# A hybrid attention and RWKV-7 block on one core: the same traced instructions, put in order by the scheduler's timeline simulation

## The chip, the cores and the metric

The kernel runs on one core of a Trainium2 chip. The metric is the device time of one execution in microseconds (us). Five engines work beside each other, each through its own instructions in a fixed order: TensorE (PE; its weight loads are shown apart as PEld), VectorE (DVE), ScalarE (ACT), GpSimd (POOL) and SyncE (SP), which here only issues DMAs. An instruction that waits holds back all that stand behind it on its engine. What order they stand in is decided when the program is built.

## The reference

One layer over x of shape (1, 2048, 1024), all in float32, cut to what is computed:

```python
h    = rms_norm(x, pre_mix_g)
proj = h @ w_in                     # 1024 -> 1536 (q,k,v) + 1792 (rwkv) + 2048 (gates)
y_a  = chunk_band_attention(q, k, v, rel_bias)      # 8 heads of 64; own chunk of 64 + 8 before
y_b  = rwkv7_time_mix(p_rwkv, ...)                  # 8 heads of 64; token shift, decay, and a scan:
#   state = state * w_t + (state @ a_t) b_t^T + v_t k_t^T ;  y_t = state @ r_t
merged = sigmoid(g_a) * (y_a @ proj_a) + sigmoid(g_b) * (y_b @ proj_b)
x = x + rms_norm(merged @ w_out, post_mix_g)
u = square(relu(rms_norm(x, pre_ffn_g) @ w_up)) @ w_down
x = x + rms_norm(u, post_ffn_g)
```

## The kernel before

**Groups.** The 2048 tokens are worked on in four groups of 512 (`G`). `run` does for each group: `phase_rwkv`, `phase_attention`, `phase_merge`, with the norm of the next group (`phase_norm`, through `after`) beside the merge. Then come the feed-forward stages, `phase_up` and `phase_down`, each twice for half of the tokens.

**Fillers.** Products are made in three passes of split operands (`mm3`, L75): each operand is the sum of a high and a low part, made by `split` (L66 on ACT, the low part L67 on DVE). `dense` makes 128 columns of the combined projection: it loads a block of weights (`wsplit`, L60 on SP), splits it (tiles `whi`, `wlo`, two buffers each), and runs 24 matmuls of 512 columns into a PSUM tile `psd` (two buffers). `gate` is such a block with a tanh behind it, `branches` multiplies by `proj_a` or `proj_b` (tile `ps_p`). Apart from their weights and buffers these matmuls depend on nothing that is under way beside them.

**RWKV, per group.** The eight heads are worked on in four pairs, two pairs at a time, as two batches.
- `rwkv_pre` makes r, k, v, the decay and the scaled operands of a pair. At its end stand the steps L411 to L424 on DVE and the matmuls `ps_A` (L470), whose evictions L479 fill the tile NA.
- `rwkv_inverse` inverts 32x32 triangular blocks by 31 pairs of small DVE steps (L503, L509) and ends in two transposes on DVE (L512, L514).
- `rwkv_blocks` needs them: `ps_t1` (L533, shown as `ps_t`), a copy on ACT (L535), `ps_t2` (L540, also shown as `ps_t`), copies on ACT (L519, L521, L542).
- `rwkv_trans` goes on for each pair in steps that each need the one before: `ps_at` (L557), `ps_w` (L564), `ps_ug` (L574), `ps_tq` (L585), `ps_s0` (L598), `ps_y` (L602), with copies on ACT and DVE between them.
- `rwkv_chunk` carries the state through eight chunks: `ps_st` (L613), then L616 on DVE, then the next `ps_st`. `rwkv_post` norms the result: L627 on ACT, L629 on DVE, L630 and L632 on POOL, L634 on DVE, then the transposes `ps_yt` (L641).

**Attention, per group.** Four pairs of heads; `att_pair` makes q, k and v by three `dense` calls, evicted by L772 to L792, and then eight blocks of 128 queries. A block is `ps_s` (scores, L817, four matmuls of 320 columns from group 1 on), `sc` on DVE (bias and minimum, L823), exp on ACT (L828), reciprocal and scaling on DVE (L830, L831), `ps_pt` (five transposes, L835), the split of those into `PTh` on ACT (L839) and `PTl` on DVE (L840). For two blocks together come twelve matmuls `ps_pv` (L847) and the sum `ya` (L850). `ps_s` and `ps_pt` have one buffer each.

**What sets the order.** The source calls the pieces in an order laid out by hand: `GATES` and `STEPS` (L33, L34) say how many gates, or how many steps of a recurrence, are called at each `between()` inside `rwkv_pre`, and `phase_rwkv` and `phase_merge` place further pieces. All calls are recorded under a `TileContext`. When it closes, a scheduler puts the recorded instructions of each engine in order: it goes through the program on a simulated machine, gives each engine, when that engine is free, the earliest recorded instruction that is ready and has its buffers, and adds the semaphores. So the simulated machine's durations decide which of two ready pieces of work goes first. In the kernel before, that machine is the default one.

## Time and profile before

| | us |
|---|---|
| median of 3 runs | 3445.39 |
| lowest and highest | 3442.23, 3445.48 |
| the profiled execution | 3440.76 |
| its span | 3439.0 |
| busy: PE / DVE / ACT / POOL | 3298.4 / 2412.6 / 1414.1 / 420.2 |
| mean granted clock of TensorE | 0.987 |

How its rows are read. Busy time is the union of an engine's instructions; a matmul's duration contains its way through the array, so the distance between the starts of two neighbours tells the rate. A row of a list of groups has line, engine, operation, tiles, sizes and count, then busy time and the mean of one in ns, then idle time ahead and what ended it. A row of the stretches has the stretch and its length, then for PE, PEld, DVE, ACT and POOL busy time and count, then the granted clock (1.00 is full), the share of the DMA engines and GB/s. A row of the timeline has start, duration, engine, line, operation and tiles, how many are merged, and in brackets the idle time ahead and what ended it. A row of the waits has the waiting engine and line, what it waited for, and the sum, the count and the longest wait.

The stretches of the span are these: the first norm and the setup to about 30 us; then four groups of some 510 us, of which RWKV takes about the first 270, attention the next 150, and the merge with the next norm the rest; the feed-forward part from about 2080 us to the end.

### The profile page before, as it was taken

What the parts mean: (1) busy time and instruction counts of PE and PEld (TensorE: products, weight loads), DVE (VectorE), ACT (ScalarE), POOL (GpSimd) and SP (SyncE); (2) the same over time, 40 slices, a digit from 0 to 9 for tenths busy, and PEclk for the clock granted to TensorE, in tenths of its full rate; (3) what the DMA queues carried; (4) which work ended last, traced back from release to release, by engine and by line L of the source; (5) the groups of instructions that cost most, each with busy time, mean ns of one, the idle gap of its engine ahead of it and who ended that gap; (6) DMA issues with size and microseconds to landing.
All of it is one profiled execution on the core that took longest, in us unless ns stands there. A gap on an engine that the chain in (4) does not pass through costs nothing. (4 is left out here: it accounts for less than half of the span.)

```text
span 3439.0 us, 50370 instructions
## 1 busy us (share of the span) xinstructions
PE 3298.4 (96%) x19233; PEld 2674.2 (78%) x19233; DVE 2412.6 (70%) x4110; ACT 1414.1 (41%) x2319; POOL 420.2 (12%) x796
## 2 busy tenths in 40 slices
PE   7999999999989999999999989999999999999998
PEld 5777777777867777877777877888788878888886
DVE  5774856766865775865775875877877788776667
ACT  4434634436644445644435634333331243331112
POOL 2210002111022110012210000111200021100001
PEclk9999999999999999999999999999999999999999
DMA  5223353225373225373224376434845374343333
GB/s 146 84 87 126 133 204 97 60 86 190 120 267 113 65 93 168 124 263 123 80 84 141 96 254 229 129 120 141 293 157 185 98 242 133 118 144 98 98 98 110
DMA packets 397864, 481.10 MB, mean 140 GB/s; under 512 B 17516, under 2 KB 304432, under 8 KB 397624
## 3 DMA queue, kind: packets, MB, share of 16 engines
q1 hardware_dynamic: 346168, 364.63, 33.4%
q0 software_dynamic: 23040, 79.71, 6.1%
q10 hardware_dynamic: 28416, 33.56, 2.8%
q8 instruction: 151, 2.47, 0.3%
q14 instruction: 89, 0.73, 0.1%
HBM read 356.16 MB, written 124.81 MB: 140 GB/s over the span
## 5 line engine op out<-in xcount | busy, mean ns | idle before, releaser
L75 PE MATMUL ps_dn<-fop 128*128 128x512 f32 x3072 | 702.6, 390 | 3.6 <-DVE u L1170 3.5
L75 PEld LDWEIGHTS ps_dn<-fop 128*128 128x128 f32 x3072 | 576.7, 188 | 125.9 <-DVE u L1170 5.8
L75 PE MATMUL psd<-hh,whi 128*128 128x512 f32 x1344 | 545.6, 406 | 14.5 <-ACT whi L66 13.6
L75 PE MATMUL psd<-hl,whi 128*128 128x512 f32 x1344 | 544.0, 405 | 0.0
L75 PE MATMUL psd<-hh,wlo 128*128 128x512 f32 x1344 | 540.9, 402 | 1.9 <-DVE wlo L67 1.8
L66 ACT CAST whi<-wraw 128x1024 fp32r<-128x1024 f32 x232 | 243.3, 1049 | 522.8 <-PE psd L75 416.7
L1170 DVE TENSOR_TENSOR u<-u,ps_dn 128x512 f32<-128x512 f32 x480 | 323.2, 685 | 148.6 <-PE ps_dn L75 147.9
L67 DVE TENSOR_TENSOR wlo<-wraw,whi 128x1024 fp32r<-128x1024 f32 x232 | 282.9, 1220 | 189.6 <-ACT whi L66 171.1
L75 PEld LDWEIGHTS psd<-hh,whi 128*128 128x128 f32 x1344 | 258.4, 192 | 68.7 <-ACT whi L66 15.5
L75 PEld LDWEIGHTS psd<-hh,wlo 128*128 128x128 f32 x1344 | 258.1, 192 | 54.0 <-DVE wlo L67 5.0
L75 PEld LDWEIGHTS psd<-hl,whi 128*128 128x128 f32 x1344 | 258.2, 192 | 50.5
L66 ACT CAST fop<-wdraw 128x1024 fp32r<-128x1024 f32 x64 | 67.0, 1047 | 425.7 <-DVE u L1170 303.3
L1091 POOL DMA_DIRECT2D ad<-r x128 | 69.2, 541 | 588.5 <-DVE r L1090 572.4
L960 PE MATMUL ps_o<-whi,mh 128*128 128x512 f32 x256 | 103.1, 410 | 15.4 <-ACT whi L66 10.0
L75 PE MATMUL ps_p<-yh,whi 128*128 128x512 f32 x256 | 103.0, 402 | 12.0 <-DVE th L931 6.7
L66 ACT CAST s12h<-s 128x1024 fp32r<-128x1024 f32 x32 | 33.7, 1055 | 184.5 <-PE ps_u L75 184.5
L823 DVE CUSTOM_DVE_ANT_0 sc<-bias,ps_s 128x640 f32<-128x640 f32 (+4 forms) x128 | 93.4, 730 | 22.6 <-PE ps_pt L835 18.4
L828 ACT ACTIVATE sc<-sc,mn 128x640 f32<-128x640 f32 (+4 forms) x128 | 97.7, 764 | 19.3 <-DVE mn L823 18.7
L839 ACT CAST PTh<-ps_pt 128x640 fp32r<-128x640 f32 (+4 forms) x128 | 79.9, 624 | 59.3 <-PE ps_pt L835 55.0
L75 PE MATMUL ps_p<-yl,whi 128*128 128x512 f32 x256 | 102.9, 402 | 0.0
L75 PE MATMUL ps_p<-yh,wlo 128*128 128x512 f32 x256 | 102.8, 402 | 0.0
L1089 ACT ACTIVATE r<-r 128x512 f32<-128x512 f32 x128 | 80.7, 630 | 53.3 <-DVE r L1088 53.1
(352 smaller groups left out, 6659.6 us busy)
## 6 DMA issues: line engine op xcount, KB each, us to landing
wraw<-in_w_in_dram SPq DMA_DIRECT2D x168, 512.0 KB
wraw<-in_w_up_dram SPq DMA_DIRECT2D x80, 512.0 KB
ad<-r POOLq DMA_DIRECT2D x128, 256.0 KB, 2.4
wdraw<-in_w_down_dram SPq DMA_DIRECT2D x64, 512.0 KB
araw<-ad SPq DMA_DIRECT2D x64, 512.0 KB
gd<-gate ACTq DMA_DIRECT2D x64, 256.0 KB
th<-gd SPq DMA_DIRECT2D x32, 512.0 KB
wraw<-in_w_out_dram SPq DMA_DIRECT2D x32, 512.0 KB
```

What stands on the lines that cost most here:

```text
L66: self.nc.scalar.copy(hi, src)
L67: self.nc.vector.tensor_tensor(lo, src, hi.bitcast(F32), ALU.subtract)
L75: mm = nc.tensor.matmul(ps, l, r, start=n == 0, stop=n == last).ins
L823: nc.vector.tensor_tensor_reduce(sc[:, 0:n], bias[:, s0:640], pss[:, c0 : c0 + n], 1.0, 3.0e38, ALU.add, ALU.min, mn,)
L828: nc.scalar.activation(sc[:, 0:n], sc[:, 0:n], AF.Exp, scale=-1.0, bias=mn, accum_out=sm)
L839: nc.scalar.copy(hv, pst[:, 0:nk])
L960: nc.tensor.matmul(ps[t], l[:, k, ts], r[:, k % 2], start=k == 0 and j == 0, stop=k == KB - 1 and j == 2)
L1089: nc.scalar.activation(r, r, AF.Relu)
L1091: nc.gpsimd.dma_start(self.ad[fb][:, th], r)
L1170: nc.vector.tensor_tensor(u[t][:, ns], u[t][:, ns], ps, ALU.add)
```

## The change

```diff
-    with tile.TileContext(nc) as tc:
+    with tile.TileContext(nc, schedule_with_timeline_sim=True) as tc:
```

One argument is added. The recorded instructions, their operands, tiles and buffers are the same. The scheduler goes through them on another simulated machine, one with a timeline of each engine and its own durations, so it meets other instructions ready at other times, and each engine's order comes out differently. The program's semaphores follow the new order. Three places show how.

**PE in an attention stage.** The first piece is from the attention of group 1 before, between two sets of transposes `ps_pt` and beyond; `psd` rows are dense matmuls for later pairs.

```order
L835 MATMUL ps_pt<-ident,sc 128x128 x5
L75 MATMUL psd<-hl,whi 128x512
L817 MATMUL ps_s<-KK,QA 128x320
L817 MATMUL ps_s<-KK,QB 128x320
L817 MATMUL ps_s<-KK,QA 128x320
L817 MATMUL ps_s<-KK,QB 128x320
L847 MATMUL ps_pv<-PTh_7790,VV 128x256 x5
L847 MATMUL ps_pv<-PTl_7791,VV 128x256
L75 MATMUL psd<-hh,wlo 128x512
L75 MATMUL psd<-hh,whi 128x512
L75 MATMUL psd<-hl,whi 128x512
L847 MATMUL ps_pv<-PTl_7791,VV 128x256 x5
```

The same kind of place in the same stage now, four blocks into a pair:

```order
L835 MATMUL ps_pt<-ident,sc 128x128 x5
L847 MATMUL ps_pv<-PTh_7790,VV 128x256 x5
L847 MATMUL ps_pv<-PTl_7791,VV 128x256
L817 MATMUL ps_s<-KK,QA 128x320
L817 MATMUL ps_s<-KK,QB 128x320
L817 MATMUL ps_s<-KK,QA 128x320
L817 MATMUL ps_s<-KK,QB 128x320
L847 MATMUL ps_pv<-PTl_7791,VV 128x256 x5
L835 MATMUL ps_pt<-ident,sc 128x128 x5
```

Before, dense matmuls stand between the links of a block; now one set of transposes follows the other with the block's own matmuls alone, and the dense ones stand in long rows ahead of or behind such runs.

**PE behind the inverse.** The first inverse of group 0 before, from the end of `ps_t1`'s filler to `ps_at` (`ps_t_1387` is `ps_t2`):

```order
L75 MATMUL psd<-hh,wlo 128x512
L75 MATMUL psd<-hh,whi 128x512
L540 MATMUL ps_t_1387<-XT,Z 32x32
L75 MATMUL psd<-hl,whi 128x512
L75 MATMUL psd<-hh,wlo 128x512
L540 MATMUL ps_t_1387<-XT,Z 32x32 x31
L557 MATMUL ps_at<-ident,AR 128x128 x4
L75 MATMUL psd<-hh,whi 128x512
```

And now, from `ps_t1` (`ps_t_1352`) on:

```order
L533 MATMUL ps_t_1352<-X_1181,NA 32x32 x32
L540 MATMUL ps_t_1387<-XT,Z 32x32 x32
L557 MATMUL ps_at<-ident,AR 128x128 x8
L564 MATMUL ps_w<-SV,AR 64x64 x16
L574 MATMUL ps_ug<-WA,XT 64x128 x16
L602 MATMUL ps_y<-SV,BR 64x64
L585 MATMUL ps_tq<-BR,GT 64x128 x8
```

Twelve dense matmuls stood between `ps_t1` and the first `ps_t2` and more behind them; now none stands in this chain.

**DVE inside the first inverse.** A piece of the same inverse now, among the small steps L503 and L509:

```order
L509 TENSOR_TENSOR X<-X,T 128x24x4
L411 TENSOR_TENSOR tk<-tk,k 128x512
L412 SCALAR_TENSOR_TENSOR ta<-ta,k 128x512
L503 TENSOR_TENSOR T<-N,X 128x115
L421 TENSOR_TENSOR BK<-tk,Ei 64x8x64 x2
L424 SCALAR_TENSOR_TENSOR r<-r,cst,tk 128x512
L418 SCALAR_TENSOR_TENSOR BK<-ta,hkk,Ei 64x8x64 x2
L509 TENSOR_TENSOR X<-X,T 128x23x5
```

Before, the end of the same inverse read:

```order
L509 TENSOR_TENSOR X<-X,T 128x16
L293 SCALAR_TENSOR_TENSOR v<-pr,cst,v 128x512
L512 STREAM_TRANSPOSE X_1181<-X 128x32x16
L514 STREAM_TRANSPOSE XD<-X_1181 128x512
L411 TENSOR_TENSOR tk<-tk,k 128x512
L412 SCALAR_TENSOR_TENSOR ta<-ta,k 128x512
```

The steps L411 to L424 of the next pair stood behind the transposes that end the inverse; now they stand inside it.

## The prediction

> **What bounds the kernel now.** First the page's busy shares, then busy time by stretch, then the list of waits, and last the timeline at the places that the new order touches.
>
> ```profile
> PE 3298.4 (96%) x19233; PEld 2674.2 (78%) x19233; DVE 2412.6 (70%) x4110; ACT 1414.1 (41%) x2319; POOL 420.2 (12%) x796
> ...
> 0.00:50.00 50.00, 28.18 (x100) 21.17 (x101) 26.77 (x61) 21.41 (x33) 11.65 (x32) 0.86 0.67 192
> 850.00:900.00 50.00, 49.65 (x289) 40.91 (x287) 41.92 (x89) 35.79 (x69) 2.85 (x9) 1.00 0.36 119
> 2200.00:2250.00 50.00, 50.00 (x222) 41.39 (x221) 40.39 (x60) 17.15 (x23) 5.51 (x11) 1.00 0.45 139
> ...
> PE ps_t L533 <- DVE X L512: 26.7, 8, 3.8
> ```
>
> TensorE is the bound nearly everywhere. It sits idle for 3439.0 - 3298.4 = 140.6 us, and 22 of those lie in the first 50 us, before any weight is there. In an attention stage (850 to 900) PE is 99% busy while DVE is 84% busy; in the feed-forward stages (2200 to 2250) PE has no idle time, and its 222 matmuls of 512 columns take 50/222 = 0.225 us each. The largest single wait is PE for the 32x32 inverse on DVE: 26.7 us in 8 waits.
>
> So the sum is easy to state. The change neither adds nor removes work; PE's work stays, and the time moves by PE's idle time alone. An order can win at most the idle time outside the start, about 120 us. What it can lose is set by how often PE is left without an independent matmul while it waits for a chain through ACT and DVE.
>
> **What the order changes.** By "filler" I mean the 512-column matmuls of `dense`, `branches` and the gates, which wait for nothing in the chain beside them. Their number is the same. In the new order they are taken earlier, as far as the buffers allow, and are gone when the chains come. I counted the fillers between one `ps_pt` group (L835) and the next in each attention stage, which has 32 such blocks and so 31 intervals. Before, no interval is empty and the least has 3. Now 21 of the 31 intervals are empty in each of the four stages, in 4 runs of 4 to 7, and the 258 fillers lie in the other ten.
>
> **Term A, attention.** What does a block without filler cost? DVE's share of a block:
>
> ```profile
> L840 DVE TENSOR_TENSOR PTl<-ps_pt,PTh 128x640 fp32r<-128x640 f32 x96 | 78.7, 819 | 8.1 <-ACT PTh L839 7.5
> L823 DVE CUSTOM_DVE_ANT_0 sc<-bias,ps_s 128x640 f32<-128x640 f32 x96 | 78.2, 815 | 20.7 <-PE ps_pt L835 16.7 <-PE ps_s L817 2.8
> L831 DVE TENSOR_SCALAR sc<-sc,rs 128x640 f32<-128x640 f32 x96 | 52.7, 549 | 1.8
> L850 DVE TENSOR_TENSOR ya<-ps_pv,y 64x256 f32<-64x256 f32 x64 | 26.5, 415 | 11.2 <-ACT y L849 9.9
> L830 DVE RECIPROCAL rs<-sm 128x1 f32<-128x1 f32 x128 | 20.2, 158 | 12.9 <-ACT sc L828 11.0
> L823 DVE DVE_READ_ACCUMULATOR2_ANT mn<- 128x1 f32 x128 | 10.4, 82 | 0.0
> ...
> L828 ACT ACTIVATE sc<-sc,mn 128x640 f32<-128x640 f32 x96 | 79.7, 830 | 12.6 <-DVE mn L823 12.4
> L828 ACT ACTIVATION_READ_ACCUMULATOR sc<-sc,mn 128x1 f32 x128 | 24.1, 189 | 0.0
> ```
>
> DVE: 0.815 + 0.082 + 0.158 + 0.549 + 0.819 + half of 0.415 (one for two blocks) = 2.63 us. PE's share, from the starts of one block in the timeline:
>
> ```profile
> 907.40 0.71 PE L835 MATMUL ps_pt<-ident,sc 128*128 128x128 f32 x5
> ...
> 907.87 0.39 PE L817 MATMUL ps_s<-KK,QA 128*128 128x320 f32 x1
> ...
> 908.54 0.39 PE L75 MATMUL psd<-hl,whi 128*128 128x512 f32 x1
> ...
> 909.69 0.76 PE L847 MATMUL ps_pv<-PTh,VV 128*128 128x256 f32 x5
> ...
> 910.41 0.39 PE L75 MATMUL psd<-hh,whi 128*128 128x512 f32 x1
> ```
>
> From start to next start: the transposes 907.87 - 907.40 = 0.47, four score matmuls 908.54 - 907.87 = 0.67, six value matmuls 910.41 - 909.69 = 0.72 (the sixth is left out above); together 1.86 us. Filled blocks hide DVE's 2.63 us, bare ones don't: the least loss is 2.63 - 1.86 = 0.77 us. It is more if the chain within a block shows. `sc` and `ps_s` of the next block may run ahead, but exp (0.83 + 0.19) must end before `rs` and the scaling, and the one `ps_pt` buffer is free only after `PTl`. Laid out in the new order of DVE (sc, PTl, rs, scale, sc of the next), with about 0.1 us for each hand-over: 0.90 for sc, 1.22 until exp is back (PTl lies inside), 0.71, 0.21 for ya: 3.04 us, a loss of 1.2. I take 1.15. The upper end adds what the new order also puts on DVE inside bare runs, the evictions of the next pair's projections:
>
> ```profile
> L775 DVE SCALAR_TENSOR_TENSOR QA<-psd,QA 64x512 fp32r<-64x512 f32 x32 | 22.0, 688 | 0.7
> L782 DVE TENSOR_TENSOR KK<-psd,KK 64x512 fp32r<-64x512 f32 x32 | 22.0, 688 | 1.3
> ```
>
> Four of the first kind (QA, QB) and two of the second per pair, 6 x 0.69 = 4.1 us, for three pairs of a stage 12 us at most; I put 8 per stage, 33 in all, into the upper end.
>
> In each of the 16 runs the first block is half done when it begins, so 84 - 16 = 68 blocks are charged: 68 x 1.15 = **+78 us**, between 68 x 0.77 = 52 and 84 x 1.15 + 33 = 130. Group 0 has smaller blocks on both engines; I leave it at the same price.
>
> **Term B, the wait for the inverse.** Each group has two inverses. PE waits 2.84 us at the end of the first, 3.84 at the second (four times each: 26.7):
>
> ```profile
> 150.53 1.20 PE L533 MATMUL ps_t<-X,NA 32*32 32x32 f32 x64 [2.84 <-DVE X L512]
> ...
> 253.03 1.20 PE L533 MATMUL ps_t<-X,NA 32*32 32x32 f32 x64 [3.84 <-DVE X L512]
> ...
> 148.77 0.74 DVE L293 SCALAR_TENSOR_TENSOR v<-pr,cst,v 128x512 f32<-128x512 f32 x1
> ...
> 151.15 0.65 DVE L411 TENSOR_TENSOR tk<-tk,k 128x512 f32<-128x512 f32 x1
> ...
> 155.04 0.75 DVE L424 SCALAR_TENSOR_TENSOR r<-r,cst,tk 128x512 f32<-128x512 f32 x1
> ...
> L67 DVE TENSOR_TENSOR wlo<-wraw,whi 128x1024 fp32r<-128x1024 f32 x232 | 282.9, 1220 | 189.6 <-ACT whi L66 171.1 <-PE ps_yt L641 16.8
> ```
>
> First inverse: between the last `ps_A` and `ps_t1` PE had 133 fillers, now 109: 24 x 0.225 = 5.4 us less to do. On DVE seven steps of `rwkv_pre` that stood behind the transposes (L411 to L424, 151.15 to 155.79, 4.6 us) now stand inside the inverse; one `wlo` (1.22), one L293 (0.74) and the L332 leave it (0.44, an estimate: four fifths of L831's 0.549 by length): +2.2 us. The wait grows from 2.84 by 7.6 to about 10.4 us: 4 x 7.6 = +30. Second inverse: 120 fillers become 152 or 153, 7 us more, so its wait goes: 4 x 3.84 = -15. The half-speed clock behind it also goes (the first row is behind a wait of 2.84 us):
>
> ```profile
> 150.00:154.00 4.00, 3.47 (x70) 2.94 (x71) 3.95 (x7) 3.30 (x6) 0.00 (x0) 0.72 0.45 130
> 254.00:257.60 3.60, 3.60 (x24) 2.89 (x17) 0.68 (x2) 3.22 (x6) 0.00 (x0) 0.53 0.50 146
> ```
>
> 3.6 us at clock 0.53 cost 1.7 us: 4 times, -7. B is 30 - 15 - 7 = **+8 us**, between -5 (DVE's moved steps find gaps) and +25 (PE comes to the second inverse sooner than counted).
>
> [...]
>
> **Term C, the chains behind the inverse.** These links of `rwkv_trans` and `rwkv_post` had fillers beside them:
>
> ```profile
> 151.26 1.24 ACT L519 COPY XT<-XD 32x512 f32<-32x512 f32 x2
> 152.51 1.25 ACT L521 COPY XT<-XD 32x512 f32<-32x512 f32 x2
> ...
> 153.78 1.18 ACT L535 COPY Z<-ps_t 32x512 f32<-32x512 f32 x2
> ...
> 160.58 1.15 PE L564 MATMUL ps_w<-SV,AR 64*64 64x64 f32 x32
> ...
> 162.78 1.96 PE L574 MATMUL ps_ug<-WA,XT 64*64 64x128 f32 x32
> ...
> 293.01 0.28 PE L613 MATMUL ps_st<-ST,TQ 64*64 64x64 f32 x4
> ...
> 296.61 0.69 DVE L634 TENSOR_TENSOR yn<-ps_y,grs 128x512 f32<-128x512 f32 x1 [2.06 <-POOL grs L632]
> ```
>
> - First half of a group, all bare from `ps_t1` into the recurrence: from the end of `ps_t1` (151.73) to ACT's last copy (154.96) and a hand-over, 3.4 us; `ps_w`'s end (161.73) to `ps_ug` (162.78), 1.05, for two pairs; some 1.5 us at `ps_at` and `ps_tq` (estimate). 7 us, less some 0.5 that PE idles there now: +6.5.
> - Second half: 24 and 22 fillers stand in the first links and hide them; `ps_w` and its like leave 3 us. New is the end: no filler between the last `ps_st` and `ps_yt`, which must await `rwkv_post` on ACT, DVE and POOL, 293.29 to 297.30 and a hand-over, 4.2 us, and about 1 for the second pair: +8.
> - The bare rounds of `rwkv_chunk` I take at nothing: a round holds one filler now, and without it the next `ps_st` can start that much sooner. At most it costs the filler's 0.225 us in some 13 rounds per group, 12 us, which goes to the upper end.
>
> C is 4 x 14.5 = **+58 us**, between 39 and 58 + 19 + 12 = 89 (each link by a third).
>
> **The rest.** The feed-forward stages keep their order but for a few groups that swap, under PE that never waits there; the merges change places with a few `ps_p` groups. PE's idle time lies there:
>
> ```profile
> 1000.00:1050.00 50.00, 41.96 (x195) 32.71 (x193) 21.43 (x22) 23.87 (x40) 8.89 (x19) 0.97 0.66 213
> 1500.00:1550.00 50.00, 42.71 (x200) 33.40 (x199) 32.21 (x30) 25.75 (x41) 14.88 (x26) 1.00 0.93 312
> 2000.00:2050.00 50.00, 40.90 (x173) 31.67 (x172) 34.83 (x48) 12.38 (x16) 3.24 (x5) 0.93 0.80 289
> ```
>
> 8.0 + 7.3 + 9.1 = 24 us in these three. The names of what is waited for there stay, so I take 0, and the same 24 in either direction for the ends.
>
> Sum: 78 + 8 + 58 = +144. The profiled execution took 3440.76 us (span 3439.0 and 1.8 around it), so **3585 us**; the median shown, 3445.4, lies 0.13% above that execution. Ends: 52 - 5 + 39 - 24 = +62, 3503 us; 130 + 25 + 89 + 24 = +268, 3709 us.
>
> **The rivals.**
> - *Faster.* The waits for the inverse all go, because PE comes late to `ps_t1` with its fillers done, and the bare stretches are hidden since ACT and DVE are further ahead. It would save 26.7 us and the slow clock behind the waits, 4 x 1.7 and 4 x 4.0 x 0.28: 3403 us. It decides itself at the price of a bare block: DVE would have to be done in 1.86 us or less. For it: PE is late at the second inverse. Against it: DVE's 2.63 us, which no order shortens.
> [...]
> - *It doesn't do what it says.* The reordered rows matter nowhere, since waits are only renamed: 3441 us. Against it stand the 21 empty intervals.
>
> **How the numbers follow.** Forecast 80%; slow clock 8%, within its range; faster 6%; no effect 3%; above 3709, 3%. Slower by over 0.2% (about what a measurement of this kernel can tell from no change) 0.91, within it 0.03, faster 0.06. The range 3503 to 3709 is set by the ends above.
>
> **What would show it.** In the changed kernel's waits, `ps_pt` L835 on DVE's `PTl` should be the longest row for PE, near 70 us; `ps_t` L533 should have 4 long waits of 8 to 12 us and no short ones; `ps_yt` L641 should wait some 4 us four times, L540 for ACT over 3 us four times. The stretches of an attention stage should read 85% PE, and the feed-forward ones 100% as before. The forecast is wrong if bare blocks follow each other in under 2.3 us, or if PE idles in the feed-forward part.

## The result, and the profile after

| | before | changed |
|---|---|---|
| median, us | 3445.4 | 3678.9 |
| lowest and highest | 3442.2, 3450.7 | 3676.5, 3681.2 |
| ratio, 95% interval | | 1.0676, 1.0663 to 1.0689 |
| span of the profiled execution | 3439.0 | 3675.3 |
| mean granted clock of TensorE | 0.987 | 0.954 |

The changed order costs 233 us, 6.8%. That lies inside the range (3503 to 3709) and above the forecast (3585): the loss forecast was 144.

The page's busy shares of the changed kernel:

```profile
PE 3383.5 (92%) x19233; PEld 2763.5 (75%) x19233; DVE 2419.0 (66%) x4110; ACT 1428.6 (39%) x2319; POOL 383.6 (10%) x796
```

The same 19233 matmuls keep TensorE busy for 85.1 us more. So the 236.3 us between the spans are 151.2 us more of idle time (291.8 against 140.6) and 85.1 us more of busy time. The mean clocks say how long the clock was halved: (1 - 0.987) x 2 x 3439 = 89 us before, (1 - 0.954) x 2 x 3675 = 338 now. By the clock records of the two traces (each holds 0.50 and 1.00 alone) TensorE was busy for 73 us of the first and for 243 us of the second. The 32 matmuls of the first `ps_ug` take 3.68 us at clock 0.50 (changed kernel, 180.81 to 184.49) and 1.96 at 1.00 (before, 162.78 to 164.74), so about half of such time is lost. Half of the 170 us between them is 85: the added busy time is slower matmuls.

The list of TensorE's waits, changed kernel (sum, times, longest):

```profile
PE ps_pv L847 <- ACT PTh L839: 54.8, 72, 0.8
PE ps_t L533 <- DVE X L512: 45.9, 4, 11.5
PE ps_s L817 <- DVE mn L823: 21.1, 29, 1.4
PE ps_s L817 <- ACT KK L762: 20.6, 3, 6.9
PE ps_yt L641 <- DVE yn L634: 15.1, 4, 3.8
...
PE ps_t L540 <- ACT Z L535: 8.6, 8, 1.9
```

The first and third rows are the bare attention blocks. `ps_t` has four long waits and no short ones, `ps_yt` four of 3.8 us. The fourth row was not foreseen: after `ps_yt` the first scores of a group wait for K.

Busy time by stretch, changed kernel (attention of groups 0 and 1, the chain behind the first inverse, the feed-forward part), and the same attention and feed-forward stretches before:

```profile
343.00:511.80 168.80, 143.79 (x610) 113.34 (x610) 95.36 (x241) 73.70 (x172) 9.70 (x31) 0.82 0.37 122
890.90:1078.60 187.70, 161.63 (x850) 133.89 (x850) 120.85 (x240) 98.31 (x178) 9.11 (x26) 0.95 0.37 121
169.50:187.00 17.50, 14.36 (x236) 12.44 (x238) 1.19 (x3) 9.29 (x20) 0.00 (x0) 0.54 0.00 1
...
2314.80:3675.00 1360.20, 1330.40 (x5869) 1096.13 (x5867) 1010.73 (x1359) 409.13 (x554) 126.36 (x228) 0.99 0.45 147
```

```profile
328.10:433.60 105.50, 103.22 (x541) 80.78 (x540) 85.08 (x232) 69.08 (x167) 7.07 (x21) 1.00 0.42 142
806.40:950.80 144.40, 141.64 (x814) 116.75 (x815) 117.57 (x239) 95.37 (x179) 9.06 (x27) 1.00 0.43 145
2096.90:3439.00 1342.10, 1318.36 (x5825) 1087.74 (x5823) 1009.45 (x1357) 406.38 (x551) 127.25 (x228) 0.99 0.45 149
```

In attention TensorE falls from 98% busy to 85% (group 0, 143.79/168.80) and 86% (group 1), and in group 0 the clock to 0.82. DVE's busy time in the stage of group 1 is nearly the same (117.6 and 120.9): it does the same work, now with TensorE waiting beside it. The feed-forward part stays at 98%.

**Where the time went.** I take as the *excess* of a matmul the time from its start to the next one's start, less the pace of its kind where nothing waits (0.227 us for 512 columns, 0.147 for scores of 320, 0.109 for a transpose, 0.119 for `ps_pv`). It holds idle time and slow clock together, and the excesses add up to 234.5 of the 236.3 us. A pair with a chain's matmul in it counts as chain, else one with an attention matmul as attention, else as filler to filler or other; from the first `ps_u` on all is feed-forward.

```
us of excess             before  changed   more
attention                  32.7    178.6  145.9
chains                     74.8    182.0  107.2
  ps_t1, first inverse     12.0     46.6   34.6
  ps_t1, second inverse    16.0      2.5  -13.4
  rest, first half                         37.2
  rest, second half                        21.4
  ps_yt to first ps_s      -1.0     26.4   27.4
filler to filler          108.2    106.4   -1.8
other                      56.9     34.0  -22.9
feed-forward               12.0     18.4    6.4
```

The first block of the kernel gives -0.3 more; the sum is 234.5.

### The profile page after: what moved, and what is told of

The parts are those of the page before. It is cut to its first block, busy times and chain, and to the rows that moved or that the text cites. A ratio compares the mean times of both kernels' runs of the same rounds, so it can differ in the third digit from the quotient of the medians.

```text
span 3675.3 us, 50455 instructions
## 1 busy us (share of the span) xinstructions
PE 3383.5 (92%) x19233; PEld 2763.5 (75%) x19233; DVE 2419.0 (66%) x4110; ACT 1428.6 (39%) x2319; POOL 383.6 (10%) x796
## 5 line engine op out<-in xcount | busy, mean ns | idle before, releaser
L823 DVE CUSTOM_DVE_ANT_0 sc<-bias,ps_s 128x640 f32<-128x640 f32 (+4 forms) x128 | 93.8, 733 | 71.8 <-PE ps_pt L835 46.9
L847 PE MATMUL ps_pv<-PTh,VV 128*128 128x256 f32 x336 | 73.3, 333 | 54.8 <-ACT PTh L839 54.8
L817 PE MATMUL ps_s<-KK,QA 128*128 128x320 f32 (+1 forms) x224 | 78.9, 358 | 47.3 <-DVE mn L823 21.1
L847 PEld LDWEIGHTS ps_pv<-PTh,VV 128*128 128x128 f32 x336 | 55.1, 213 | 74.5 <-ACT PTh L839 70.7
L960 PE MATMUL ps_o<-wlo,mh 128*128 128x512 f32 x256 | 103.6, 405 | 3.7 <-DVE wlo L67 3.6
```

Of the source, the lines that this page charges most:

```text
L817: nc.tensor.matmul(pss[:, c0 + lo_ : c0 + lo_ + w], q[:, par, qs], Kv[:, k0 + lo_ : k0 + lo_ + w], start=i == 0, stop=i == 1,)
L823: nc.vector.tensor_tensor_reduce(sc[:, 0:n], bias[:, s0:640], pss[:, c0 : c0 + n], 1.0, 3.0e38, ALU.add, ALU.min, mn,)
L847: nc.tensor.matmul(pv, st, x[:, kt], start=i == 0, stop=i == len(terms) - 1)
L960: nc.tensor.matmul(ps[t], l[:, k, ts], r[:, k % 2], start=k == 0 and j == 0, stop=k == KB - 1 and j == 2)
```

## The experiments

All runs use one tool: order edges, which make one instruction stand behind another on the same engine and add no semaphore. With a table of one engine's order the scheduler is held to that order there, and orders the rest itself. E7 and E10 hold all engines to the changed order, the others hold what is said.

```diff
         Block(tc, aps, out[0]).run()
+        keep_order(tc, ORDER)
...
+    for row in table:                      # instructions of one engine, in order
+        for a, b in zip(row, row[1:]):
+            tc.add_manual_dep(ins[b], a, info, reason="issue order")
```

The tables do not hold the step L823 on DVE, which is made from its record only when the program is built. The engines that are not held come out in orders of their own, which need be neither kernel's. The excess of eight runs, each from its profiled execution (E2's took 3794.6 us), to be read beside the table above:

| us | attention | chains | filler to filler | other | feed-forward | median, ratio (interval) |
|---|---|---|---|---|---|---|
| E1, PE of before | 77.3 | 115.7 | 109.4 | 48.0 | 38.4 | 3544.1, 1.0287 (1.0271 to 1.0302) |
| E2, PE of the change, rest plain | 212.4 | 181.7 | 164.6 | 55.0 | 24.5 | 3780.2, 1.0981 (1.0956 to 1.1006) |
| E3, PE of before in attention | 75.3 | 183.4 | 94.2 | 38.3 | 16.5 | 3563.9, 1.0344 (1.0326 to 1.0362) |
| E4, PE of before in RWKV | 193.3 | 113.8 | 121.1 | 41.5 | 18.1 | 3647.0, 1.0586 (1.0570 to 1.0602) |
| E5, PE and DVE of before | 73.0 | 86.6 | 151.3 | 70.7 | 18.1 | 3556.1, 1.0317 (1.0303 to 1.0331) |
| E6, DVE of before | 206.4 | 103.8 | 162.0 | 110.3 | 27.6 | 3771.9, 1.0948 (1.0931 to 1.0965) |
| E9, PE, DVE, ACT of before | 48.9 | 75.2 | 138.9 | 59.9 | 11.3 | 3490.5, 1.0135 (1.0118 to 1.0152) |
| E12, these and SP of before | 46.6 | 74.3 | 112.1 | 56.7 | 9.7 | 3459.2, 1.0039 (1.0027 to 1.0052) |

### E1 and E2: TensorE's order alone

E1 is the changed kernel with all of TensorE held to the order of before; E2 is the kernel before with TensorE held to the changed order.

> The changed kernel, with TensorE held to the order that it had before (all its matmuls, order edges without semaphores); the other engines are ordered by the timeline simulation. Theory: TensorE's order alone makes the loss, since it decides whether a matmul without dependencies stands beside a waiting chain; the time comes back to 3445, within 25 us (3420 to 3470). Rival: the new orders of VectorE, ScalarE and the DMA queue carry a part of it by themselves (seven steps of rwkv_pre inside the inverse, evictions between the links of a block); then 3500 or more.

> The kernel before, with TensorE held to the changed kernel's order and the other engines ordered by the plain simulation. Theory that TensorE's order alone does it: 3679, within 30 us. Rival, that the other engines' orders carry a part: the bare blocks stay (about 86 us over before), but the evictions inside the bare runs and the longer inverse wait go, 30 and 35 us: 3615 or less.

E1 came to 3544, where the rival had it (3500 or more): 135 of 233 us come back, 99 stay. The theory that TensorE's order is everything falls. E1's waits:

```profile
PE ps_t L533 <- DVE X L512: 56.5, 8, 8.5
PE ps_p L75 <- DVE th L931: 41.8, 7, 14.3
...
PE ps_pv L847 <- ACT PTh L839: 3.9, 9, 0.6
```

The wait for PTh, the bare blocks' mark, is down from 54.8 to 3.9 us, so these are TensorE's order. But the inverse is waited for longer than before (56.5 against 26.7): TensorE's fillers stand where they stood, and DVE still has its new steps inside the inverse. E2 came to 3780, slower than either kernel and outside both expectations. An order taken from one simulated run and set among engines ordered by another loses twice: the bare blocks stay, and `psd` waits 46 us for evictions.

```profile
PE ps_pv L847 <- ACT PTh L839: 51.0, 65, 0.8
PE psd L75 <- DVE QA L775: 46.2, 12, 5.9
```

### E3 and E4: one stage at a time

TensorE's order of before from the first `ps_s` to the last `ps_pv` of each group (E3), or from the first `ps_A` to the last `ps_yt` (E4); all else as changed.

> The changed kernel with TensorE's order of before in the four attention stages alone, from the first ps_s to the last ps_pv of each. The excess over a matmul's own pace that the two traces show around the attention's matmuls is 33 us before and 179 after, 146 more. Theory, that stages add up: 3679 - 146 = 3533, within 25 us. Rival, that fillers taken back for the attention are missed elsewhere and the loss only moves: above 3580.

> The changed kernel with TensorE's order of before in the four RWKV stages alone, from the first ps_A to the last ps_yt of each. The excess around the matmuls of the chains is 75 us before and 182 after, 107 more, of which 27 lie between ps_yt and the first ps_s. Theory, that stages add up: 3679 - 107 = 3572 if the gap before the first ps_s goes too, 3599 if it stays. Rival, that the loss only moves to the attention, which then has fewer fillers: above 3630.

E3: 3564, 115 us back where 146 were expected. The attention's excess fell from 178.6 to 75.3 and the chains' stayed at 183.4, so the attention's order is a loss of its own and does not only move. It came out between the two expectations: 43 us stay in attention. E4: 3647, only 32 back. The chains gained 68 us, but attention lost 15 more and the other fillers 15 more; the rival's figure (above 3630) came true. In E4 the inverse is waited for 56.0 us, as in E1.

### E5, E6, E9 and E12: the other engines

> The changed kernel with the orders of before on TensorE and VectorE, all of them; ScalarE, GpSimd and the DMA queue are ordered by the timeline simulation. With TensorE's order alone 98 us stayed, and most of the waits that stayed are for VectorE (56.5 for the inverse, 41.8 for th). Theory, that the two orders together are the loss: 3445, within 20 us. Rival, that what stays is the other queue's (weights, biases and th loaded at other times): 3490 or more, with the 41.8 us for th still in the waits.

> The changed kernel with VectorE's order of before alone; TensorE's is left to the timeline simulation. Theory, that the parts add up: TensorE's order of before took 135 us off and 98 stayed, so VectorE's alone takes 98 off: 3581, within 25. Rival, that an order is only as good as its match on the other engine (TensorE's new order under VectorE's plain one gave 3780): 3640 or more, perhaps above 3679.

> The changed kernel with the orders of before on TensorE, VectorE and ScalarE; GpSimd and the DMA queue stay with the timeline simulation. With TensorE's and VectorE's orders of before 110 us were left. Theory, that ScalarE's order holds them (TensorE still waited 15 us for PTh, 8 us more for the inverse's last cast or its start, and VectorE 25 us more for ScalarE and its DMAs): 3445 to 3470. Rival, that the DMA queue's order holds them (th and weights asked for late): 3530 or more.

> The changed kernel with the orders of before on TensorE, VectorE, ScalarE and the DMA queue (SP); GpSimd alone stays with the timeline simulation. With the first three, 45 us were left, and in the trace TensorE waited 30 us for th, whose loads stand in the DMA queue. Theory, that the DMA queue's order is the last part: 3445, within 8 us. Rival, that GpSimd's order or the order edges themselves cost something: 3460 or more.

E5 gave 3556, in the rival's range: DVE's order on top of TensorE's brings nothing (12 us slower), though the wait for the inverse falls. E6, DVE's order alone, gave 3772, worse than the change itself. TensorE's order was free there and came out as neither kernel's: 43% of its matmuls stand at their place of before, 47% at that of the changed kernel. So what single engines' orders give does not add up, and E6 doesn't say what DVE's order is worth beside the changed order of TensorE. With ScalarE's order 66 us come back (E9, 3490, between its two expectations), with the DMA queue's 31 more (E12, 3459). The waits of E5, and then of E9, show what went where:

```profile
PE ps_t L533 <- DVE X L512: 34.2, 8, 4.7
PE ps_p L75 <- DVE th L931: 33.7, 6, 10.8
...
PE psd L75 <- DVE wlo L67: 15.3, 5, 3.5
PE ps_pv L847 <- ACT PTh L839: 15.1, 20, 1.6
```

```profile
PE ps_p L75 <- DVE th L931: 30.3, 5, 10.6
PE ps_t L533 <- DVE X L512: 26.9, 8, 3.8
```

ScalarE's order took away the waits for PTh and `wlo` (the splits begin on ScalarE), and brought the inverse to 26.9 us, where it was before (26.7). The wait for `th`, whose load stands in the DMA queue, stayed at 30.3 and went to 11.6 in E12. E12 ends 13 us above before, between its two expectations; 13.9 us of excess lie in attention, where L823 is the step that no edge holds. In E12's trace all other DVE steps stand as before, and 66 of the 128 L823 stand up to three places off. That this is the cause was not tried apart; GpSimd's order was free too.

### E7 and E10: is it the wait or the clock?

The changed kernel with all orders kept, and with matmuls that nothing reads in the gaps of the first inverse: 44 ahead of `ps_t1` (E7), and in E10 9 more ahead of the first `ps_t2` and 3 ahead of the first `ps_ug`.

```diff
+        for _ in range(warm):
+            m = nc.tensor.matmul(ps.rearrange("p q c t -> p (q c t)"), self.h[0][:, 0, 0:P], self.h[0][:, 1], start=True, stop=True)
```

> The changed kernel, all orders kept, with 44 matmuls of 512 columns ahead of ps_t1 in the first inverse of each group; nothing reads what they write (ps_t1 overwrites it). They take 44 x 0.227 = 10.0 us of the 11.48 us that TensorE waits there. Theory, that the wait sets the half clock and the chain behind it pays: ps_t1 to ps_ug run 15 us at half clock now, with full clock some 5 us less per group: 3679 - 20 = 3659. Rival, that the thin matmuls of the chain hold the clock down by themselves: at most ps_t1's 0.7 us per group, 3676 or no change.

> The changed kernel, all orders kept, with matmuls that nothing reads in each gap of the first pair's chain behind the first inverse: 44 ahead of ps_t1, 9 ahead of the first ps_t2 (9 x 0.227 = 2.0 us of a wait of 1.9 to 2.7), 3 ahead of the first ps_ug (0.7 of 0.8). Theory, that half clock itself is a price: with the gaps filled, ps_t1, ps_t2, ps_at, ps_w and ps_ug run at their full-clock times (1.2, 1.2, 0.7, 1.0, 2.0 in place of 1.9, 1.9, 1.1, 2.0, 3.7), 4 to 5 us per group: 3679 - 18 = 3661. Rival, that ScalarE's copies set the pace of this chain and TensorE's speed is hidden behind them: 3675 or more.

E7: 3681.6 (1.0685, 1.0664 to 1.0706), no change, as its rival had it. E10: 3668.9 (1.0670, 1.0638 to 1.0702), 10 us less than the change by the medians, with intervals that overlap: between its two expectations, and no gain clear of the noise. The timelines of the chain, changed kernel, E7, E10:

```profile
169.46 1.91 PE L533 MATMUL ps_t<-X,NA 32*32 32x32 f32 x64 [11.48 <-DVE X L512]
173.24 0.31 PE L540 MATMUL ps_t<-XT,Z 32*32 32x32 f32 x2 [1.87 <-ACT Z L535]
...
180.81 3.68 PE L574 MATMUL ps_ug<-WA,XT 64*64 64x128 f32 x32 [0.78 <-ACT WA L565]
```

```profile
157.92 10.13 PE L531 MATMUL ps_t<-hh 128*128 128x512 f32 x44
169.49 1.20 PE L536 MATMUL ps_t<-X,NA 32*32 32x32 f32 x64 [1.44 <-DVE X L512]
173.36 0.31 PE L543 MATMUL ps_t<-XT,Z 32*32 32x32 f32 x2 [2.67 <-ACT Z L538]
...
180.93 3.68 PE L577 MATMUL ps_ug<-WA,XT 64*64 64x128 f32 x32 [0.78 <-ACT WA L568]
```

```profile
170.01 1.20 PE L539 MATMUL ps_t<-X,NA 32*32 32x32 f32 x64 [1.44 <-DVE X L512]
171.14 2.33 PE L526 MATMUL ps_t<-hh 128*128 128x512 f32 x9
173.89 0.24 PE L547 MATMUL ps_t<-XT,Z 32*32 32x32 f32 x2 [0.42 <-ACT Z L541]
...
180.95 1.96 PE L582 MATMUL ps_ug<-WA,XT 64*64 64x128 f32 x32
```

In E7 `ps_t1` takes 1.20 us, as before at clock 1.00, in place of 1.91 at 0.50. But the 0.7 us only lengthens the wait for ScalarE's copy (2.67 against 1.87), and behind it the chain is slow again: `ps_ug` 3.68 us, as in the changed kernel at clock 0.50. In E10, with that gap filled too, `ps_ug` takes 1.96, as before at clock 1.00. From the start of `ps_t1` to the end of the first `ps_ug` it is 14.2 us on the mean of the four groups in the changed kernel, 12.7 in E10. So the half clock is worth some 1.5 us per group in this part of the chain, as far as the gaps were filled: in group 0 of E10 the second four of `ps_at` still take 1.12 us and `ps_w` 1.97, as long as at clock 0.50 in the changed kernel (1.12 and 1.97). The rest of the chain's length stays with `ps_t1`, `ps_t2` and `ps_ug` at 1.20, 1.19 and 1.96 us, and by the waits of the changed kernel (`Z` 1.87 and 0.29, `WA` 0.78 us) it is ScalarE's copies. The half clock further on and in the other stages was not filled in any run.

### E8 and E11: a faster kernel?

E8 is the kernel before with TensorE's changed order only between the stages, where the changed trace had 25 us less excess, and in the feed-forward part, where it had 6 more. E11 keeps the order of before and moves fillers to the two inverses; fillers and chains keep their own sequences. TensorE's order of E11 against that of before, for one group:

```diff
 L75 MATMUL psd (the last of the fillers ahead of the first ps_t1)
+L75 MATMUL psd x13
 L533 MATMUL ps_t_1352<-X_1181,NA 32x32
...
+L75 MATMUL psd x17
 L533 MATMUL ps_t (second inverse)
...
 L641 MATMUL ps_yt (the last of the group)
-L75 MATMUL psd x30
```

> The kernel before, with TensorE's order of the changed kernel only from the end of each attention stage to the next group's first ps_A, and in the feed-forward part. Between two such fillers and around the merge's matmuls the changed trace has 25 us less excess than before, and 6 more in the feed-forward part. Theory, that stages add up: 3445 - 19 = 3426, a kernel faster than both. Rival, that the gain belongs to the other engines' orders and TensorE's order without them costs: 3450 or more.

> The kernel before, with TensorE's order of before in which 13 filler matmuls more stand ahead of the first ps_t1 of each group and 17 more ahead of the second (13 x 0.225 = 2.9 us, 17 x 0.225 = 3.8 us: the waits there), taken from the 42 or more between ps_yt and the first ps_s; the fillers keep their sequence, the chains theirs. Theory: the eight waits (26.7 us) and the half clock behind them go, 26.7 + 8 x 1.7 = 40 us less some 4 us per group for the start of attention, whose cover shrinks: 3445 - 24 = 3421. Rival, that the operands of the fillers taken forward come too late (each needs its weights and a free psd), or that the start of attention costs all of it: 3440 or more.

E8: 3459.4 (1.0040, 1.0027 to 1.0053), 0.4% slower: TensorE's changed order alone doesn't bring the 19 us (25 - 6) less of those parts. What does was not tried. E11: 3471.1 (1.0083, 1.0068 to 1.0098), 0.8% slower, in the rival's range. Its theory's first half came true: `ps_t` L533 is no longer among the waits. In its place, from E11's waits:

```profile
PE ps_s L817 <- ACT KK L762: 27.9, 3, 9.6
```

The start of attention costs up to 9.6 us in three of the groups, 27.9 in all, where 4 per group were reckoned with. This is the wait that the changed kernel has too (20.6 us, longest 6.9), made here on purpose by taking its cover away. No version faster than the kernel before was found.

## Why the prediction came out as it did

- **Direction and bound: right.** The work is the same (19233 matmuls, DVE 2412.6 and 2419.0 us), and the time moved by TensorE's waits and its clock. That it moves "by PE's idle time alone" was wrong: 85 of the 236 us are matmuls at half clock. That the total stayed inside the range is in part luck: term A passed its own upper end and a whole term was missed, and the room came from the upper ends of the other terms and from the 18 us of the rest.
- **Term A: right in mechanism, too small: 78 forecast, 146 measured, 130 its upper end.** The 84 empty intervals show as forecast, and a bare block costs what was laid out. Bare run in group 1, changed kernel, timeline of TensorE:

```profile
935.55 0.77 PE L835 MATMUL ps_pt<-ident,sc 128*128 128x128 f32 x5
937.10 0.85 PE L847 MATMUL ps_pv<-PTh,VV 128*128 128x256 f32 x5 [0.78 <-ACT PTh L839]
...
939.08 0.71 PE L835 MATMUL ps_pt<-ident,sc 128*128 128x128 f32 x5
940.63 0.39 PE L847 MATMUL ps_pv<-PTh,VV 128*128 128x256 f32 x1 [0.84 <-ACT PTh L839]
...
941.72 0.74 PE L835 MATMUL ps_pt<-ident,sc 128*128 128x128 f32 x5
```

  From set to set 3.53 and 2.64 us, on the mean 3.09, where 3.04 was laid out. What was mis-sized stands beside it. All 84 intervals pay, not 68. The 76 of them without an eviction have 110.8 us of excess, 1.46 each in place of 1.15; in group 1, at full clock, it is 1.35. The other 8 hold evictions of the next pair's projections and have 30.2 us, 3.8 each: this was put at 8 us per stage and into the upper end only, but it happens twice in every stage. DVE, two of these steps in the changed kernel:

```profile
946.86 0.55 DVE L831 TENSOR_SCALAR sc<-sc,rs 128x640 f32<-128x640 f32 x1
947.42 0.69 DVE L775 SCALAR_TENSOR_TENSOR QB<-psd,QA 64x512 fp32r<-64x512 f32 x1
948.13 0.69 DVE L775 SCALAR_TENSOR_TENSOR QA<-psd,QA 64x512 fp32r<-64x512 f32 x1
948.75 0.69 DVE L782 TENSOR_TENSOR KK<-psd,KK 64x512 fp32r<-64x512 f32 x1
949.46 0.42 DVE L850 TENSOR_TENSOR ya<-ps_pv,y 64x256 f32<-64x256 f32 x1
949.91 0.82 DVE L823 CUSTOM_DVE_ANT_0 sc<-bias,ps_s 128x640 f32<-128x640 f32 x1
```

  Between the scaling and the next block's `sc` stand 2.5 us of other work. That this is TensorE's order is shown for 103 us of the 146 by E3; 24 more came back with ScalarE's order (73.0 in E5, 48.9 in E9), and 14 stayed to the end (E12).
- **The name of the wait was wrong.** `ps_pt` on `PTl` was to be the longest row; it is `ps_pv` on `PTh`, since in the new order `ps_pv` stands right behind `ps_pt`. The chain is the same, TensorE meets it one link earlier.
- **Term B: right in mechanism, +8 forecast, some +14 measured, and a part not charged.** The waits cost 21 us more, 15 were forecast: the first was put at 10.4 and is 11.48; the second went. The half clock behind the second inverse went too, as forecast. The fillers there had 1.8 to 2.0 us of excess per group and have 0.24 now, some 7 us in all, which the table counts under filler to filler. The stretch from the second `ps_t1` of group 0, changed kernel, where 0.53 stood before:

```profile
290.50:294.10 3.60, 3.60 (x75) 3.07 (x75) 1.23 (x1) 2.61 (x4) 0.00 (x0) 1.00 0.26 80
```

  What the sum didn't charge is the slow clock behind the first inverse. The clock is halved in its long wait, from 161.80 on, and stays so through the chain (0.54 from 169.5 to 187.0). What that costs stands in term C's first half. That DVE's moved steps lengthen the first wait is borne out by E1 and E4, where it is 8.5 us with TensorE's fillers back.
- **Term C: right in sum, 58 forecast, 58.6 measured** (37.2 and 21.4), but by luck, with the halves off in opposite ways: 26 and 32 were forecast. The first half is longer in part by its half clock (by E10 some 1.5 us per group); in the second `ps_yt` waited 3.8 us four times as forecast, the rest was too dear. L540 was to wait over 3 us four times; its longest is 1.9.
- **Missed: the start of attention, 27 us.** "No filler between the last `ps_st` and `ps_yt`" was counted; that none stands behind `ps_yt` either was not. ScalarE, changed kernel, group 2:

```profile
1463.86 0.56 ACT L646 ACTIVATE yf<-ps_yt,gbo,gwo 64x256 f32<-64x256 f32 x1
1464.45 0.59 ACT L772 ACTIVATE QA<-psd 64x512 fp32r<-64x512 f32 x1
...
1468.36 1.03 ACT L762 CAST KK<-kr 128x1024 fp32r<-128x1024 f32 x1
```

  Behind `ps_yt` come ScalarE's steps for y, then Q, then the cast of the old K, and only then the first scores. 42 to 66 fillers, 9.5 us and more, covered this before. E11 shows this price in the order of before.
- **The rest: 0 forecast, -18 measured,** within its bounds of 24. Some 7 of it are term B's half clock. E8 shows that TensorE's order there brings no gain by itself.
- **The rivals.** The slow clock, given 8%, is true in part: bare blocks of group 0 run at half clock for half of their time (0.82 in the stage), those of the other groups for a sixth. One place of the stage shows the price: from set to set it takes 3.51 us at full clock in group 1 (from 974.85), 4.94 and 4.63 at mean clocks of 0.68 and 0.73 in groups 2 and 3 (from 1559.53 and 2142.83). But the intervals with evictions take 6.32 us in these three groups at mean clocks from 0.62 to 0.85: there DVE and ScalarE set the pace. The clock is also at 0.50 behind the waits of 11.48 and 3.78 us of group 0 (from 161.80 and 332.47), which the sum did not charge. In the chain behind the first inverse, filling the gaps brings 10 us by the medians (E10), none clear of the noise: little of the half clock shows in the time there, though small matmuls that wait for ScalarE run at half speed as well (`ps_ug` 3.68 and 1.96 us).
- **What no term held:** the new orders of ScalarE and the DMA queue. By E9 and E12 they are worth 66 and 31 us on top of TensorE's and DVE's orders. Added in another sequence the shares may differ, as E6 warns.

## What to carry to other kernels

Independent matmuls are a fixed stock: count, for every chain, how many the new order leaves beside it, up to the first matmul behind the chain, and price each empty place by the length of the other engines' chain, with all that is queued on them there. An order that comes from one simulated run is a fit of all engines to each other; one engine's part of it, put among another run's, can be worse than either. So compare whole orders, and look for a gain in the chains' length before moving their cover about.

## What the runs showed of the hardware that was not expected

In the changed kernel TensorE's clock falls to 0.50 also without a long wait ahead of it. Stretches of the changed kernel, three of group 1, two of group 0 and two of group 3, each following the one ahead of it in its group:

```profile
936.60:940.00 3.40, 2.69 (x20) 2.46 (x20) 2.41 (x6) 1.85 (x5) 0.00 (x0) 1.00 0.03 9
940.00:943.40 3.40, 1.83 (x10) 1.30 (x10) 3.03 (x8) 3.02 (x6) 0.00 (x0) 1.00 0.00 0
943.50:946.80 3.30, 3.02 (x10) 2.32 (x10) 2.84 (x5) 3.24 (x7) 0.00 (x0) 0.50 0.73 233
...
206.20:209.60 3.40, 2.57 (x29) 2.18 (x28) 3.28 (x11) 0.00 (x0) 0.00 (x0) 1.00 0.00 0
209.60:213.00 3.40, 3.40 (x26) 2.80 (x25) 3.10 (x10) 0.00 (x0) 0.00 (x0) 0.50 0.00 0
...
2267.80:2271.20 3.40, 1.81 (x7) 1.21 (x8) 3.40 (x5) 0.57 (x1) 0.72 (x1) 1.00 1.02 358
2271.30:2274.60 3.30, 3.30 (x17) 2.71 (x16) 2.15 (x3) 1.05 (x1) 0.00 (x0) 1.00 1.02 393
```

A stretch in which TensorE was busy for 1.83 of 3.4 us, with no wait above 1 us in it, was followed by one at clock 0.50. In the clock records of the two traces 18 half-clock times before and 41 in the changed kernel last 3.41 us or a multiple of it (3.41 to 23.89), and one more in each, the last, runs to the end; the starts at 151.72 and 254.12 before lie 30 x 3.413 apart. The busy time of one such stretch doesn't decide: behind 79% busy (from 936.60) the clock stayed full, behind 76% (from 206.20) it fell, behind 53% (from 2267.80) it stayed full, and behind 54% (from 940.00) it fell. What decides stays open.
